# Homes of matmul operands modulo 128 bytes in a split-precision macaron block on one NeuronCore

## The chip, the cores and the metric

The kernel runs on one core of a Trainium2 chip. The metric is the device time of one execution in microseconds.

## The reference

One inference step of a diffusion backbone of two layers with `D_MODEL` 1024, on 128 context tokens and 512 latent tokens, all in float32. Each layer is a macaron block with adaLN modulation and norms on both sides:

```python
mod = adaln(c, w_mod[l], b_mod[l])
z = ffn_half(z, mod, 0, norm_w[l, 0], norm_w[l, 1], ffn_w1[l, 0], ffn_w2[l, 0])
h = modulate(rms_norm(z, norm_w[l, 2]), mod, 3)
q, k, v, gu, gv, pl = project(h, w_in[l])
...
out = merge_heads(attn, gu, gv, pl, w_spatial[l], b_spatial[l], w_pool[l], pool_scale[l], w_out[l])
z = z + mod[:, 5][:, None, :] * rms_norm(out, norm_w[l, 3])
z = ffn_half(z, mod, 6, norm_w[l, 4], norm_w[l, 5], ffn_w1[l, 1], ffn_w2[l, 1])
```

where `ffn_half` is x + 0.5 · gate · rms_norm(SwiGLU(h)), with `(silu(g) * u) @ w2` and [g, u] = h @ w1, and D_FF = 2816. The context tokens take the same path with weights in common and a conditioning vector of their own. The tokens' keys and values of the context are outputs too.

## The kernel before, in words

The tokens lie in five tiles of 128: group A holds tiles 0 and 1 (256 columns), group B tiles 2, 3 and 4 (384 columns; tile 4 is the context). There are six stages, three to a layer: 0, 2, 3 and 5 are feed-forward halves (`ffn_stage`), 1 and 4 are the mixing stages.

Every float32 operand of a matmul is split into a high part rounded to the format that TensorE multiplies and a low part, the difference (`split`, line 359: the high part on ACT at line 360, the low part on DVE at line 361). A product is then three matmuls that add into one PSUM bank: high by high, weight high by activation low, weight low by activation high. All of them are recorded at line 365 (`mm`), so the profile tells them apart by their operands: in `PS<-h0hi,whi` the first name is the moving operand (its columns stream through), the second the stationary one (it is loaded by an LDWEIGHTS, PEld in the profile).

The weights come by DMA into `raw`, are split into `whi` by ACT (line 328) and `wlo` by DVE (line 330), and wait in pools eight deep.

- The first product of a feed-forward half (`ffn1`, line 553): weight slices are stationary and the transposed, modulated tokens `h0` (group A) and `h1` (group B) move, as tiles of eight rows k of 256 or 384 columns in a high and a low part. For f in blocks of the hidden width, some f's run for group A alone ahead of the others (24 f's of 48 matmuls in all four stages together), while group B's tokens are still being made.
- In stages 2, 3 and 5, 49 blocks are done with seven products instead of eight (`ffn1_blocks`, line 657), which need sums of token parts: `S1` (256 columns) and `SZ` (384 columns), made by `sums`. Each product is twelve matmuls: products 0 and 1 use h0, 2 and 5 SZ, 3 S1, 4 and 6 h1.
- In stage 0 the f's that are not done for A alone take h0 and h1 in turn (15 f's of 48 of each), and `h1` is two columns wider there, for tokens whose shift comes late.
- The second product (`ffn2`, line 739, and `mm_tok`, line 698): the activations are stationary and the weights move, 512 columns at a time. The activation's high part `ahi` and low part `alo` are made by `ensure`: ahi in a pool of four, alo in the buffer of the previous activation (lines 759 and 760):

```python
hi = self.asp.tile([P, WB], F32R, name="ahi")
...
lo = self.ap.tile([P, wid], F32, name="alo", tag=f"act{g}{order[len(sp) - 1]}").bitcast(F32R)
...
def stat(f):
    ensure(order.index(f) + 1)
    return sp[f]
```

- The projections of the mixing stages use h0 and h1 as stationary operands, with moving weights.
- Beside the second products, DVE also adds up rows of the modulation matrices (line 434, `acc` from `wmt`), whose transfers are issued by SP (line 429).

The order on each engine is set by a scheduler that goes by priorities: each generator step gets a priority, and `sums` runs behind the stage's matmuls by `S_LAG` and `S_RATE` (line 38). Tiles are allocated in the order in which the pools and tags appear; `c1` is the pool of tiles that live for the whole program, `actp` the pool of activations of one stage. `new_h` (line 475) gives the tiles of h, and `boundary` (line 533) calls it at the end of a stage.

Of the kernel before, what the change touches and what calls it, by code (L numbers as in the profile page):

```python
# [8 lines left out]
F32 = mybir.dt.float32  # L9
F32R = mybir.dt.float32r  # L10
# [5 lines left out]
P = 128  # L16
D = 1024
KD = 8
# [5 lines left out]
GA = (0, 1)  # L24
GB = (2, 3, 4)
WA = 256
WB = 384
# [7 lines left out]
ADA_RATE2 = 0.7  # L35

BLOCKS = (2, 3, 5)
S_LAG, S_RATE = 30, 0.5
FREE = 1
MISC0 = (8, 9, 10, 11, 0, 1, 2, 3, 4, 5, 6, 7)  # L40
TAIL_A, TAIL_B, TAIL = 4, 1, 3
# [120 lines left out]
class Builder:  # L162
    def __init__(self, ctx, tc, a, n_stage=6):
        self.tc = tc
        self.nc = tc.nc
        self.a = a
        self.n_stage = n_stage
        pool = lambda name, bufs, **kw: ctx.enter_context(tc.tile_pool(name=name, bufs=bufs, **kw))
        self.c1 = pool("c1", 1)
        self.rawp = pool("raw", 5)  # L170
        self.wp = pool("wsp", 8)
        self.xp = pool("xp", 3)
        self.tmpp = pool("tmp", 4)
        self.stp = pool("st", 6)
        self.mdp = pool("md", 2)
        self.psp = pool("ps", 1, space=bass.MemoryType.PSUM)
        self.PS = self.psp.tile([P, 4096], F32, name="PS")
        self.ring = {}
        self.turn = {}
        self.drp = pool("dr", 1, space=bass.MemoryType.DRAM)  # L180
        self.xd = [self.drp.tile([P, D], F32, name=f"xd{t}", tag=f"xd{t}") for t in range(NT)]
        self.units = []
        self.plan()
        self.n_dma = 0
        self.n_split = 0
        self.n_use = 0
        self.dmas = []
        self.raws = {}
        self.spl = {}
        self.kept = {}  # L190
        self.pins = []
        self.lo_pool = 0
        self.xt = {}
        self.hT = {}
        self.md = {}
        self.rowd = {}
        self.pairs = {}
        self.kept_tmp = {}

    def bank(self, i):  # L200
# [175 lines left out]
    def setup(self):  # L376
        nc, a, c1 = self.nc, self.a, self.c1
        ct = c1.tile([P, C_W], F32, name="ct")
        cc = c1.tile([P, 2, KD], F32, name="cc")
        nc.sync.dma_start(cc[:, 0, :], a["c"].rearrange("b (p k) -> p (b k)", k=KD))  # L380
        nc.sync.dma_start(cc[:, 1, :], a["c_ctx"].rearrange("(p k) -> p k", k=KD))
        nc.sync.dma_start(ct[:, 0:C_COS], a["consts"][:, 0:C_COS])
        self.ident = ct[:, C_ID:C_ID + P]
        self.mhalf = ct[:, C_INVW + 2:C_INVW + 3]
        self.ct = ct
        self.identr = c1.tile([P, P], F32R, name="identr")
        nc.vector.tensor_copy(self.identr, self.ident)
        bf = c1.tile([P, 3, P], BF16, name="bf")
        nc.vector.tensor_copy(bf[:, 0, :], self.ident)
        self.bf = bf  # L390
        self.identb, self.maskL, self.maskR = bf[:, 0, :], bf[:, 1, :], bf[:, 2, :]
        self.ones = c1.tile([P, P], F32, name="ones")
        nc.vector.memset(self.ones, 1.0)
        self.cc = c1.tile([P, 2, KD], F32, name="ccs")
        nc.scalar.activation(self.cc, cc, AF.Silu)
        self.selc = c1.tile([P, 2], F32, name="selc")

    def setup_late(self):
        nc, a = self.nc, self.a
        mk = self.c1.tile([P, 2, P], F32, name="mk")  # L400
        nc.sync.dma_start(mk, a["consts"][:, C_ML:C_ALL].rearrange("p (a b) -> p a b", a=2))
        nc.sync.dma_start(self.ct[:, C_COS:C_W], a["consts"][:, C_COS:C_W])
        nc.vector.tensor_copy(self.bf[:, 1:3, :], mk)
        self.jk = mk.rearrange("p a b -> p (a b)").bitcast(BF16)
# [68 lines left out]
        self.nc.sync.dma_start(x, src)  # L473
        self.xt[t] = x

    def new_h(self, g):
        w = (WA, WB + 2)[g]
        return tuple(self.c1.tile([P, KD, w], F32R, name=f"h{g}{n}", tag=f"h{g}{n}") for n in ("hi", "lo"))

    def hcol(self, t):  # L480
        g = 0 if t in GA else 1
# [50 lines left out]

    def boundary(self, s, tiles, post, pre, cost, skew=3):
        if pre:
            self.hT[0 if tiles[0] in GA else 1] = self.new_h(0 if tiles[0] in GA else 1)
        gens = [self.bnd_steps(s, t, post, pre) for t in tiles]
        w = 0
        done = [False] * len(gens)
        while not all(done):
            for i, g in enumerate(gens):  # L540
                if not done[i] and w >= skew * i:
                    try:
                        next(g)
                    except StopIteration:
                        done[i] = True
            w += 1
            yield cost
# [194 lines left out]
    def ffn2(self, l, i, g, last=False):  # L742
        wid = (WA, WB)[g]
        sp = {}

        order = list(range(NF))
        if g:
            order = order[NF - KEEP_C:] + order[:NF - KEEP_C]

        def ensure(f):  # L750
            while len(sp) <= min(f, NF - 1):
                q = order[len(sp)]
                hi = self.asp.tile([P, WB], F32R, name="ahi")
                a = self.act[q, g]
                if len(sp):
                    lo = self.ap.tile([P, wid], F32, name="alo", tag=f"act{g}{order[len(sp) - 1]}").bitcast(F32R)
                else:
                    lo = self.asp.tile([P, WB], F32R, name="ahi")[:, 0:wid]
                self.nc.scalar.activation(hi[:, 0:wid], a, AF.Copy)  # L759
                self.nc.vector.tensor_tensor(lo, a, hi[:, 0:wid].bitcast(F32), ALU.subtract)  # L760
                sp[q] = (hi, lo)

        def stat(f):
            ensure(order.index(f) + 1)
            return sp[f]
        ensure(0)
        yield from self.mm_tok(lambda c, n: ("w2", l, i, c, n), (GA, GB)[g], order, stat, late=1 if g else 0, tail=(TAIL_A, TAIL_B, TAIL)[g + last])
# [523 lines left out]
    def ffn_stage(self, s, l, i, pend):  # L1291
        tc = self.tc
        last = s == self.n_stage - 1
        q = STG[s]
# [2 lines left out]
        early = list(range(max(0, na - KEEP_F)))  # L1297
        block = lambda pool, name: lambda *n: pool.tile([P, D], F32, name=name + "".join(map(str, n)))
        rows = [sum([self.rows(n) for n in ns if n < self.n_stage], []) for ns in ({0: (0, 1)}.get(s, ()), ADA_LATE[s])]
        with tc.tile_pool(name="actp", bufs=1, reuse_waits="tile") as ap, ExitStack() as late:  # L1300
            self.ap = ap

            def pools():
                self.asp, self.wmp, self.accsp = (late.enter_context(tc.tile_pool(name=n, bufs=b, reuse_waits="tile"))
                                                  for n, b in (("asp", 4), ("wmp", 3), ("accsp", 1)))
# [142 lines left out]
```

## Time and profile before

| | |
|---|---|
| median of 3 runs | 2399.22 us (2397.61 to 2403.58) |
| the profiled execution | 2398.8 us |
| its span | 2397.0 us |
| mean granted clock of TensorE | 0.993 |
| busy: TensorE / weight loads / DVE / ACT / GpSimd | 2317.4 / 2063.2 / 1829.1 / 1117.4 / 394.4 us |
| matmuls | 13304 |
| read from HBM, over the span | 341.50 MB, 149 GB/s with what is written |

The span is the time from the first to the last instruction that the profiler recorded; the execution's own time has 1.8 us more around it. TensorE's busy time is a modelled one: matmuls overlap, and a group's mean duration is longer than the time from one start to the next. To know what a matmul takes in a stream, one reads the starts in the timeline, not the durations.

### The profile page before, as it was taken

Reading aid. Unit: us, or ns where it says so; the run is one execution under the profiler, and the core shown is the slowest. Engines: PE = TensorE matmul, PEld = TensorE weight load, DVE = VectorE, ACT = ScalarE, POOL = GpSimd, SP = SyncE. Lnnn points to the kernel's source line nnn. Section 1 sums busy time; section 2 is a strip of 40 time slices with the busy share of each in tenths; the row PEclk is TensorE's granted clock in tenths of the full one; section 3 lists DMA queues with packets and bytes.
Section 4 is the critical chain, followed back from the end, with each engine's and each line's share of the span. In section 5 each row is a group of like instructions: output and inputs, shape, how many; then the busy total and the mean of one; then the engine's idle time right before and its main releaser. Section 6 shows DMA issues by size and latency. Waiting matters only on the chain.

```text
span 2397.0 us, 37303 instructions
## 1 busy us (share of the span) xinstructions
PE 2317.4 (97%) x13304; PEld 2063.2 (86%) x13304; DVE 1829.1 (76%) x2914; ACT 1117.4 (47%) x2309; POOL 394.4 (16%) x432
## 2 busy tenths in 40 slices
PE   8999999999999999999999999999999889999998
PEld 6999897777778999997789999877777789999887
DVE  5568678977776778889966888899958774788754
ACT  5422224444766444444453444544455563444543
POOL 2000000305324200000240000021545370000000
PEclk9999999999999999999999999999999999999999
DMA  9357667654325522348654222577622354222542
GB/s 295 113 174 242 197 194 249 230 163 127 107 71 155 170 80 80 88 137 266 219 181 121 86 82 80 197 227 245 213 73 62 106 172 137 75 85 71 187 156 93
DMA packets 330481, 360.07 MB, mean 150 GB/s; under 512 B 20451, under 2 KB 239843, under 8 KB 330294
## 3 DMA queue, kind: packets, MB, share of 16 engines
q1 hardware_dynamic: 326694, 344.58, 46.0%
q10 hardware_dynamic: 3600, 13.11, 1.4%
q8 instruction: 104, 1.70, 0.3%
q14 instruction: 83, 0.68, 0.1%
HBM read 341.50 MB, written 16.12 MB: 149 GB/s over the span
## 4 chain that ended last, share of the span: by engine, by line
PE 72%; DVE 13%; DMA 5%; issue 5%; POOL 2%; ACT 2%; SPq 1%; DVEq 0%; ACTq 0%; POOLq 0%
PE PS L365 70%; DVE wlo L330 3%; DVE acc L434 3%; DMA wmt<-in_w_mod 3%; DMA raw<-in_ffn_w 2%; DVE alo L760 1%; DVE ast L1057 1%; PE PS L443 1%; PE PS L1080 1%; POOL tmp L515 1%; DVE x L504 1%; DVE tl L361 1%; POOL wlo L330 0%; ACT pt L1063 0%; DVE h1lo L361 0%
## 5 line engine op out<-in xcount | busy, mean ns | idle before, releaser
L328 ACT ACTIVATE whi<-raw 128x512 fp32r<-128x512 f32 x668 | 417.0, 630 | 537.4 <-PE PS L365 387.8
L330 DVE TENSOR_TENSOR wlo<-raw,whi 128x512 fp32r<-128x512 f32 x614 | 455.4, 755 | 207.9 <-ACT whi L328 199.2
L365 PE MATMUL PS<-whi,ahi 128*128 128x512 f32 x920 | 354.6, 393 | 0.0
L365 PE MATMUL PS<-h1hi,whi 128*128 128x384 f32 (+1 forms) x1016 | 342.5, 338 | 2.2 <-ACT h1hi L360 2.1
L365 PE MATMUL PS<-h1hi,wlo 128*128 128x384 f32 (+1 forms) x1016 | 344.0, 339 | 0.0
L365 PE MATMUL PS<-h1lo,whi 128*128 128x384 f32 (+1 forms) x1016 | 343.4, 338 | 0.0
L365 PE MATMUL PS<-wlo,ahi 128*128 128x512 f32 x880 | 342.8, 391 | 0.0
L328 ACT ACTIVATE whi<-tmp 128x512 fp32r<-128x512 f32 x294 | 185.7, 633 | 256.7 <-PE PS L365 189.2
L365 PE MATMUL PS<-h0hi,whi 128*128 128x256 f32 x1016 | 289.7, 286 | 9.2 <-DVE act L596 8.6
L434 DVE SCALAR_TENSOR_TENSOR acc<-wmt,ccs,acc 128x1024 f32<-128x1024 f32 x224 | 279.7, 1278 | 24.3 <-DMA wmt<-in_w_mod 24.1
L365 PE MATMUL PS<-whi,alo 128*128 128x512 f32 x840 | 274.1, 396 | 21.0 <-DVE alo L760 21.0
L365 PE MATMUL PS<-h0hi,wlo 128*128 128x256 f32 x1016 | 289.2, 285 | 0.0
L365 PE MATMUL PS<-h0lo,whi 128*128 128x256 f32 x1016 | 288.9, 285 | 0.0
L330 DVE TENSOR_TENSOR wlo<-tmp,whi 128x512 fp32r<-128x512 f32 x294 | 201.5, 686 | 78.8 <-ACT whi L328 73.1
L365 PEld LDWEIGHTS PS<-whi,alo 128*128 128x128 f32 x840 | 155.0, 188 | 69.4 <-DVE alo L760 31.3
L365 PEld LDWEIGHTS PS<-h0hi,whi 128*128 128x128 f32 x1016 | 193.7, 191 | 20.0 <-DVE act L596 10.0
L365 PEld LDWEIGHTS PS<-whi,ahi 128*128 128x128 f32 x920 | 172.9, 188 | 39.5 <-ACT ahi L759 1.7
L365 PE MATMUL PS<-sz,whi 128*128 128x384 f32 x784 | 200.8, 337 | 0.0
L365 PEld LDWEIGHTS PS<-h0hi,wlo 128*128 128x128 f32 x1016 | 193.7, 191 | 4.3 <-issue 3.4
L365 PEld LDWEIGHTS PS<-wlo,ahi 128*128 128x128 f32 x880 | 165.3, 188 | 36.2
L365 PEld LDWEIGHTS PS<-h0lo,whi 128*128 128x128 f32 x1016 | 194.2, 191 | 1.8 <-issue 1.7
L365 PEld LDWEIGHTS PS<-h1hi,whi 128*128 128x128 f32 x1016 | 190.9, 188 | 2.8 <-ACT h1hi L360 2.8
(239 smaller groups left out, 4213.3 us busy)
## 6 DMA issues: line engine op xcount, KB each, us to landing
raw<-in_ffn_w SPq DMA_DIRECT2D x540, 256.0 KB
wmt<-in_w_mod SPq DMA_DIRECT2D x136, 512.0 KB
tmp<-in_ffn_w SPq DMA_DIRECT2D x98, 512.0 KB
raw<-in_w_in SPq DMA_DIRECT2D x80, 256.0 KB
xd<-x ACTq DMA_DIRECT2D x25, 512.0 KB
x<-xd SPq DMA_DIRECT2D x25, 512.0 KB
raw<-in_w_out SPq DMA_DIRECT2D x64, 128.0 KB
mdG<-rowG SPq DMA_DIRECT2D x12, 512.0 KB
```

The costliest lines, as they stand in the source:

```text
L328: self.nc.scalar.activation(hi, r, AF.Copy)
L330: eng.tensor_tensor(lo, r, hi.bitcast(F32), ALU.subtract)
L361: i1 = (eng or self.nc.vector).tensor_tensor(lo, src, hi.bitcast(F32), ALU.subtract)
L365: self.nc.tensor.matmul(out, w, m, start=start, stop=stop)
L434: nc.vector.scalar_tensor_tensor(accs[s], w, self.cc[:, s, k:k + 1], prev, ALU.mult, ALU.add)
L443: nc.tensor.matmul(ps[32 * q:32 * q + 32, :], self.ones[:, 0:32], accs[q // 2][:, 512 * (q % 2):512 * (q % 2) + 512], start=True, stop=Tru ...
L504: nc.vector.scalar_tensor_tensor(x, tmp, r, x, ALU.mult, ALU.add)
L515: nc.gpsimd.tensor_tensor(tmp[:, hs], tmp[:, hs], self.md["T", st][:, hs], ALU.add)
L760: self.nc.vector.tensor_tensor(lo, a, hi[:, 0:wid].bitcast(F32), ALU.subtract)
L1057: nc.vector.tensor_reduce(mx, S, AX.X, ALU.max)
L1080: nc.tensor.transpose(ps[:, w * c + P * j:w * c + P * j + P], pt[:, n * j + P * (c0 + c):n * j + P * (c0 + c) + P], self.ident)
```

## The change

There are three parts. First, it places three 64-byte tiles that nothing reads ("gap", "gap1", "gap2"), and makes the rows of h1 1536 bytes apart instead of 1544 (stage 0 keeps 1544). With this the addresses of the matmuls' operands within a partition, taken modulo 128 bytes, are as follows in the two built programs:

| operand | before | changed |
|---|---|---|
| weights `whi`, `wlo` | 64 | 64 |
| `h0`, high and low part | 64 | 0 |
| `h1`, high part, row k | 64 + 8k | 64 (stage 0: 64 + 8k) |
| `h1`, low part, row k | 8k | 64 (stage 0: 64 + 8k) |
| `S1` | 0 | 0 |
| `SZ` | 0 | 64 |
| activations, `ahi`, `alo` | 0 | 64 |
| `wmt`, `acc` | 0 | 64 |

Second, `ensure` is asked for activation parts two blocks ahead instead of one. Third, `S_LAG` and `S_RATE`, which set the priority of the token sums, go from 30 and 0.5 to 400 and 0.45.

```diff
--- before.py
+++ after.py
@@ -35,7 +35,7 @@
 ADA_RATE2 = 0.7
 
 BLOCKS = (2, 3, 5)
-S_LAG, S_RATE = 30, 0.5
+S_LAG, S_RATE = 400, 0.45
 FREE = 1
 MISC0 = (8, 9, 10, 11, 0, 1, 2, 3, 4, 5, 6, 7)
 TAIL_A, TAIL_B, TAIL = 4, 1, 3
@@ -195,6 +195,7 @@
         self.md = {}
         self.rowd = {}
         self.pairs = {}
+        self.gap = None
         self.kept_tmp = {}
 
     def bank(self, i):
@@ -394,6 +395,7 @@
         self.cc = c1.tile([P, 2, KD], F32, name="ccs")
         nc.scalar.activation(self.cc, cc, AF.Silu)
         self.selc = c1.tile([P, 2], F32, name="selc")
+        c1.tile([P, 16], F32, name="gap")
 
     def setup_late(self):
         nc, a = self.nc, self.a
@@ -473,9 +475,12 @@
         self.nc.sync.dma_start(x, src)
         self.xt[t] = x
 
-    def new_h(self, g):
-        w = (WA, WB + 2)[g]
-        return tuple(self.c1.tile([P, KD, w], F32R, name=f"h{g}{n}", tag=f"h{g}{n}") for n in ("hi", "lo"))
+    def new_h(self, g, late=False):
+        w = (WA, WB + 2 * late)[g]
+        if g == 1 and self.gap is None:
+            self.gap = self.c1.tile([P, 16], F32, name="gap1")
+        flat = [self.c1.tile([P, KD * (WA, WB + 4)[g]], F32R, name=f"h{g}{n}", tag=f"h{g}{n}") for n in ("hi", "lo")]
+        return tuple(v[:, 0:KD * w].rearrange("p (k q) -> p k q", k=KD) for v in flat)
 
     def hcol(self, t):
         g = 0 if t in GA else 1
@@ -532,7 +537,8 @@
 
     def boundary(self, s, tiles, post, pre, cost, skew=3):
         if pre:
-            self.hT[0 if tiles[0] in GA else 1] = self.new_h(0 if tiles[0] in GA else 1)
+            g = 0 if tiles[0] in GA else 1
+            self.hT[g] = self.new_h(g, not post)
         gens = [self.bnd_steps(s, t, post, pre) for t in tiles]
         w = 0
         done = [False] * len(gens)
@@ -761,7 +767,7 @@
                 sp[q] = (hi, lo)
 
         def stat(f):
-            ensure(order.index(f) + 1)
+            ensure(order.index(f) + 2)
             return sp[f]
         ensure(0)
         yield from self.mm_tok(lambda c, n: ("w2", l, i, c, n), (GA, GB)[g], order, stat, late=1 if g else 0, tail=(TAIL_A, TAIL_B, TAIL)[g + last])
@@ -1297,8 +1303,9 @@
         early = list(range(max(0, na - KEEP_F)))
         block = lambda pool, name: lambda *n: pool.tile([P, D], F32, name=name + "".join(map(str, n)))
         rows = [sum([self.rows(n) for n in ns if n < self.n_stage], []) for ns in ({0: (0, 1)}.get(s, ()), ADA_LATE[s])]
-        with tc.tile_pool(name="actp", bufs=1, reuse_waits="tile") as ap, ExitStack() as late:
+        with tc.tile_pool(name="gap", bufs=1, reuse_waits="tile") as gp, tc.tile_pool(name="actp", bufs=1, reuse_waits="tile") as ap, ExitStack() as late:
             self.ap = ap
+            gp.tile([P, 16], F32, name="gap2")
 
             def pools():
                 self.asp, self.wmp, self.accsp = (late.enter_context(tc.tile_pool(name=n, bufs=b, reuse_waits="tile"))
```

The order of the instructions on each engine, taken from the built programs, is the same before and in the change but for DVE and ACT at the start of stage 0. The line numbers of the changed program are up to six higher.

DVE at the start of stage 0, before; h1lo is the low part of group B's tokens, wlo that of a weight tile, and the rows on ahi and tmp belong to the late shift:

```order
28 L330 TENSOR_TENSOR wlo<-raw,whi 128x512 x4
29 L361 TENSOR_TENSOR h1lo<-PS,h1hi 128x4x128
30 L330 TENSOR_TENSOR wlo<-raw,whi 128x512 x5
31 L361 TENSOR_TENSOR acc_679<-acc_365,acc_679 99x512
32 L330 TENSOR_TENSOR wlo<-raw,whi 128x512
33 L361 TENSOR_TENSOR h1lo<-PS,h1hi 128x4x128
34 L330 TENSOR_TENSOR wlo<-raw,whi 128x512 x5
35 L361 TENSOR_TENSOR h1lo<-PS,h1hi 128x4x128 x3
36 L330 TENSOR_TENSOR wlo<-raw,whi 128x512
37 L1253 COPY ahi<-PS 128x16
38 L1266 SCALAR_TENSOR_TENSOR tmp<-h0hi,ahi,h0lo 128x256 x5
39 L361 TENSOR_TENSOR h1lo<-ahi,h1hi 128x8x2
```

The same place in the change:

```order
28 L331 TENSOR_TENSOR wlo<-raw,whi 128x512 x4
29 L362 TENSOR_TENSOR h1lo<-PS,h1hi 128x4x128
30 L331 TENSOR_TENSOR wlo<-raw,whi 128x512 x5
31 L362 TENSOR_TENSOR acc_684<-acc_370,acc_684 99x512
32 L331 TENSOR_TENSOR wlo<-raw,whi 128x512 x6
33 L362 TENSOR_TENSOR h1lo<-PS,h1hi 128x4x128 x4
34 L331 TENSOR_TENSOR wlo<-raw,whi 128x512
35 L1259 COPY ahi<-PS 128x16
36 L1272 SCALAR_TENSOR_TENSOR tmp<-h0hi,ahi,h0lo 128x256 x4
37 L362 TENSOR_TENSOR h1lo<-ahi,h1hi 128x8x2
```

The split of h1lo that stood alone between one and five splits of weights (row 33 before) now stands behind all six, together with the three others; one more h1lo split (128x8x2) has moved ahead of one of the five steps on tmp.

DVE in the ffn2 of stage 0, before; alo is the low part of an activation, acc a sum of modulation rows:

```order
276 L434 SCALAR_TENSOR_TENSOR acc_3743<-wmt,ccs 128x1024
277 L760 TENSOR_TENSOR alo<-act_261,ahi 128x256
278 L330 TENSOR_TENSOR wlo<-raw,whi 128x512 x2
279 L434 SCALAR_TENSOR_TENSOR acc_3742<-wmt,ccs,acc_3742 128x1024
280 L434 SCALAR_TENSOR_TENSOR acc_3743<-wmt,ccs,acc_3743 128x1024
281 L760 TENSOR_TENSOR alo<-act_263,ahi 128x256
282 L330 TENSOR_TENSOR wlo<-raw,whi 128x512 x3
283 L760 TENSOR_TENSOR alo<-act_265,ahi 128x256
```

The same place in the change:

```order
274 L436 SCALAR_TENSOR_TENSOR acc_3753<-wmt,ccs 128x1024
275 L766 TENSOR_TENSOR alo<-act_266,ahi 128x256
276 L331 TENSOR_TENSOR wlo<-raw,whi 128x512 x2
277 L436 SCALAR_TENSOR_TENSOR acc_3752<-wmt,ccs,acc_3752 128x1024
278 L436 SCALAR_TENSOR_TENSOR acc_3753<-wmt,ccs,acc_3753 128x1024
279 L766 TENSOR_TENSOR alo<-act_268,ahi 128x256
280 L331 TENSOR_TENSOR wlo<-raw,whi 128x512 x3
281 L766 TENSOR_TENSOR alo<-act_270,ahi 128x256
```

Nothing has moved: only the numbers in the names of buffers are higher, and each alo stands behind the same accumulation step and ahead of the same weight splits.

DVE in the group-B pass of stage 2, where the token sums are made, before; s and sz are S1 and SZ, and the step on act is part of a block's combination of products:

```order
740 L330 TENSOR_TENSOR wlo<-raw,whi 128x512
741 L642 TENSOR_TENSOR s_8621<-s_8621,h0lo 128x1024
742 L361 TENSOR_TENSOR h1lo<-PS,h1hi 128x4x128
743 L611 TENSOR_TENSOR tmp<-tmp,h0hi 128x512
744 L361 TENSOR_TENSOR sz_8236<-tmp,sz_8235 128x4x128
745 L596 TENSOR_TENSOR act_7753<-act_7753,PS 128x256
746 L529 TENSOR_TENSOR tmp<-tmp,PS 128x512
```

The same place in the change:

```order
738 L331 TENSOR_TENSOR wlo<-raw,whi 128x512
739 L648 TENSOR_TENSOR s_8632<-s_8632,h0lo 128x1024
740 L362 TENSOR_TENSOR h1lo<-PS,h1hi 128x4x128
741 L617 TENSOR_TENSOR tmp<-tmp,h0hi 128x512
742 L362 TENSOR_TENSOR sz_8247<-tmp,sz_8246 128x4x128
743 L602 TENSOR_TENSOR act_7764<-act_7764,PS 128x256
744 L534 TENSOR_TENSOR tmp<-tmp,PS 128x512
```

Here, too, only the numbers in the names differ.

## Rows read from the trace of the kernel before

**Rows 1.** The page: busy us, share, instructions; shares of the chain that ended last.

```profile
PE 2317.4 (97%) x13304; PEld 2063.2 (86%) x13304; DVE 1829.1 (76%) x2914; ACT 1117.4 (47%) x2309; POOL 394.4 (16%) x432
...
PE 72%; DVE 13%; DMA 5%; issue 5%; POOL 2%; ACT 2%; SPq 1%; DVEq 0%; ACTq 0%; POOLq 0%
```

**Rows 2.** TensorE's waits, by releaser: us in total, times, longest.

```profile
PE PS L365 <- DVE alo L760: 21.0, 22, 1.8
```

**Rows 3.** Stretches: length, busy PE, PEld, DVE, ACT, POOL; clock, DMA share, GB/s.

```profile
860.00:1060.00 200.00, 200.00 (x1331) 200.00 (x1330) 169.12 (x315) 95.39 (x191) 0.00 (x0) 1.00 0.28 79
430.00:500.00 70.00, 66.13 (x293) 50.90 (x295) 66.25 (x80) 30.57 (x58) 19.54 (x13) 1.00 0.66 218
2260.00:2390.00 130.00, 130.00 (x570) 106.66 (x569) 67.57 (x109) 55.45 (x109) 3.44 (x8) 1.00 0.41 132
```

**Rows 4.** Groups of TensorE: count | busy us, mean ns | idle before, releasers.

```profile
L365 PE MATMUL PS<-whi,ahi 128*128 128x512 f32 x920 | 354.6, 393 | 0.0
...
L365 PE MATMUL PS<-wlo,ahi 128*128 128x512 f32 x880 | 342.8, 391 | 0.0
L365 PE MATMUL PS<-h1hi,whi 128*128 128x384 f32 (+1 forms) x1016 | 342.5, 338 | 2.2 <-ACT h1hi L360 2.1
L365 PE MATMUL PS<-h0hi,whi 128*128 128x256 f32 x1016 | 289.7, 286 | 9.2 <-DVE act L596 8.6 <-ACT act L586 0.6
...
L365 PE MATMUL PS<-whi,alo 128*128 128x512 f32 x840 | 274.1, 396 | 21.0 <-DVE alo L760 21.0
L365 PE MATMUL PS<-sz,whi 128*128 128x384 f32 x784 | 200.8, 337 | 0.0
...
L365 PE MATMUL PS<-whi,h0hi 128*128 128x512 f32 x160 | 62.6, 409 | 5.4 <-ACT qf L887 2.6 <-DVE pl L883 1.6 <-ACT h0hi L360 1.0
```

**Rows 5.** Timeline of TensorE, S1 moving: start us, duration us, operation.

```profile
966.67 0.41 PE L365 MATMUL PS<-s,whi 128*128 128x256 f32 x2
...
967.03 0.39 PE L365 MATMUL PS<-s,whi 128*128 128x256 f32 x2
...
967.93 0.28 PE L365 MATMUL PS<-s,wlo 128*128 128x256 f32 x1
968.05 0.34 PE L365 MATMUL PS<-h1hi,whi 128*128 128x384 f32 x1
```

**Rows 6.** Timeline of TensorE, h0 moving, first and last of 95.

```profile
1981.44 0.28 PE L365 MATMUL PS<-h0lo,whi 128*128 128x256 f32 x1
...
1992.59 0.28 PE L365 MATMUL PS<-h0hi,wlo 128*128 128x256 f32 x1
```

**Rows 7.** Timeline, 512 columns: stationary h0, activations, h1; first and last of each.

```profile
535.58 0.40 PE L365 MATMUL PS<-wlo,h0hi 128*128 128x512 f32 x1
...
545.81 0.39 PE L365 MATMUL PS<-whi,h0hi 128*128 128x512 f32 x1
...
1106.78 0.63 PE L365 MATMUL PS<-whi,alo 128*128 128x512 f32 x2
...
1143.88 0.39 PE L365 MATMUL PS<-wlo,ahi 128*128 128x512 f32 x1
...
1919.17 0.40 PE L365 MATMUL PS<-whi,h1lo 128*128 128x512 f32 x1
...
1937.27 0.39 PE L365 MATMUL PS<-whi,h1lo 128*128 128x512 f32 x1
```

**Rows 8.** Timeline, 384 columns: h1 moving (first, last of 197), then SZ.

```profile
812.11 0.34 PE L365 MATMUL PS<-h1hi,whi 128*128 128x384 f32 x1
...
846.48 0.34 PE L365 MATMUL PS<-h1hi,whi 128*128 128x384 f32 x1
...
913.88 0.51 PE L365 MATMUL PS<-sz,whi 128*128 128x384 f32 x2
...
916.00 0.41 PE L365 MATMUL PS<-s,whi 128*128 128x256 f32 x2
```

**Rows 9.** The page's costliest groups: DVE's split of weights.

```profile
L330 DVE TENSOR_TENSOR wlo<-raw,whi 128x512 fp32r<-128x512 f32 x614 | 455.4, 755 | 207.9 <-ACT whi L328 199.2
```

## The prediction

> **What bounds the kernel now.** First the busy times and the chain that ended last [rows 1]: TensorE is busy for 2317.4 of the span's 2397.0 us, and 72% of the chain is its own work, with 13% of DVE and 5% of transfers. Where it works, little stops it, so what one matmul takes is the kernel's time. The second view is the list of what TensorE waits for. Its largest entry in the matmuls of line 365 is the low part of an activation, "alo" of line 760: 21.0 us in 22 waits [rows 2]. The third view, by stretches, tells which stages have room [rows 3]. In the seven-product blocks of stage 2 (860 to 1060 us) both TensorE and its weight loads are busy without a gap at a granted clock of 1.00, the 2.4 GHz level; in the last ffn2 (2260 to 2390) TensorE has no gap either; in the first ffn2 (430 to 500) it is busy for 66.13 of 70 us, and DVE for 66.25, so DVE sets the pace there. The fourth view groups the matmuls by operands [rows 4] and gives the counts below.
>
> The change names two homes, so the next thing to read is what one matmul takes at each. The durations in the groups overlap (a 256-column matmul shows 286 ns and the next starts after 119), so I read starts from the timeline, the distance from one start to the next.
> - 256 columns, S1 moving (home 0, weights at 64): three at 120 ns each, from 966.67 to 967.03, then nine in 1.02 us, 113.3 ns each [rows 5].
> - 256 columns, h0 moving (home 64, weights at 64): 94 intervals from 1981.44 to 1992.59, 118.6 ns each [rows 6].
> - 512 columns: activations stationary (home 0, weights moving at 64), 162 intervals from 1106.78 to 1143.88, 229.0 ns; h0 stationary (home 64), 44 intervals, 232.5 ns; h1 stationary (mixed homes), 78 intervals, 232.05 ns [rows 7].
> - 384 columns: h1 moving (mixed homes), 196 intervals, 175.4 ns; SZ moving (home 0), 12 in 2.12 us, 176.7 ns [rows 8].
>
> Equal columns, different times: the cheaper one of each pair has its two operands in opposite 64-byte halves of 128, the dearer one in the same half. At 384 columns the pairing shows nothing.
>
> **The change, part by part.** The sum is made against the profiled execution, 2398.8 us; the median of the runs is 0.4 us above it, too little to matter.
>
> 1. *h0 moves from 64 to 0, opposite to the weights.* It is then where S1 is now. There are 1016 matmuls of each of three products, 3048 [rows 4]: 1176 in blocks (49 blocks of 24), 1152 in the parts of group A alone (24 f's of 48), 720 in stage 0 where they alternate with h1. A block: 24 × 118.6 = 2846 ns now; as S1, 3 × 120 + 21 × 113.3 = 2739; 107 ns saved, × 49 = **−5.2 us**. TensorE has no gap in the blocks, so this is all on the path. Group A alone: 1152 × 5.3 ns = 6.1 us. But its end is where TensorE waits, 8.6 us for DVE's gate "act" of line 596 and 2.1 for h1hi [rows 4]; what is late next is the same product at the same time. The ends are 0 and −6.1; I take half, **−3.0**. In stage 0 an h0 matmul stands beside one of h1 and never repeats; ends 0 and 720 × 5.3 = −3.8; I take **0**, since the first three of S1 behind a matmul of another operand gain nothing either.
> 2. *The activation parts move from 0 to 64, to the half of the weights.* 920 + 880 + 840 = 2640 matmuls [rows 4] go from 229.0 to h0's 232.5: 3.5 ns each, 9.2 us if all is on the path, 2.3 a stage. The last ffn2 has no gap and pays its 2.3 whole. In the other three TensorE waits 21.0 us for DVE's alo [rows 2]: slower matmuls there use time that is waited anyway. Ends 0 and 6.9; I take a third, 2.3. Together **+4.6**.
> 3. *h0 stationary in the mixing stages*, 3 × 160 = 480 matmuls [rows 4], goes the other way, 480 × −3.5 = −1.7; some end at waits; **−1.2**.
> 4. *h1 and SZ to 64.* 3048 h1 matmuls and 1176 of SZ move, 384 columns, and 720 with h1 stationary. Both kinds lie at 175 to 177 ns now, whichever the home, so **0**. Upper end: 3048 × (176.7 − 175.4) = +4.0. Lower end: S1's settled rate by columns, 113.3 × 1.5 = 170.0, or 5.4 × 3048 = −16.5. I stand far from the latter because SZ is already opposite the weights, as S1 is, and doesn't get there.
> 5. *Activation parts two ahead, and the sums' lag.* In the order of the built programs every alo stands between the same accumulation steps and weight splits, and every sum between the same neighbours: **0**. What covers this is the full DVE [rows 3], whose queue is served in that order however early the request is made. If the request did come sooner, the 21.0 us would be the most to gain.
> 6. *The start of stage 0:* one h1lo split stands behind five more weight splits of 0.755 us [rows 9]. If TensorE waited for that split alone it would lose 3.8 us. But three h1lo splits stood behind the same five before and still do, and the pass needs all of them: **0**, with the weight parts sooner by one split.
> 7. No instruction, transfer or queue entry is added: the gaps are memory. The rows of h1 that are 1536 instead of 1544 bytes apart change no count; **0**.
>
> Sum: −5.2 − 3.0 + 4.6 − 1.2 = −4.8, so **2394.0 us**; its own range, from half of each uncertain term, 2390 to 2399. A measurement of this kernel can tell about 0.3% from no change, 7.2 us; this case lies within it.
>
> **The rivals.**
> *B, the stationary side is free.* All of ffn2's 6.9 us in three stages vanish in the 21.0 us of waits, and h0 gains everywhere: −5.2 − 6.1 − 1.7, half of stage 0's 3.8 (−1.9), +2.3 in the last stage: −12.6, **2386.2**. For it: alo's waits are three times the cost. Against: 22 waits among 1980 matmuls mean that most of those matmuls run in streaks, as the 162 intervals do, and the waits for act follow the early end of group A. With h1 settling as well it would go below 2380.
> *C, homes don't matter and the change does nothing.* The differences would come from what runs beside: then 2398.8. Against it stand 113.3 and 118.6 ns for the same 256 columns, both at the 2.4 GHz level. The Trainium skill speaks for C (TensorE: Matmul & The Clock Gate, "Step-by-step: what each phase is for"): one read port of SBUF feeds the moving operand and another one the weight load, so loading doesn't take bandwidth from the running matmul. If that were all, opposite and equal halves would cost alike; the rows of S1 and h0 disagree.
> *D, the predecessor decides; slower.* S1 settles behind SZ, and both are now at home 0. If a streak settles only behind a matmul of its own home, h0 (behind h1, at 64) gains nothing, and S1 (behind SZ, now at 64) goes from 115.0 (1.38 us over 12) to 118.6: 49 × 12 × 3.6 ns = +2.1. ffn2's cost, between the +4.6 taken and the full 9.2, is +6.9. Sum +9.0, **2407.8**. It decides if S1's group takes over 1.41 us in the changed trace and h0's stays at 118. Against it: S1 settles after three matmuls, so the predecessor's trace is short.
>
> **How the numbers follow.** The forecast A 0.38, B 0.36, C 0.08, D 0.18. Faster by over 0.3% is B, 0.36; within it are A and C, 0.46; slower is D, 0.18. The range 2379 to 2408 leaves out half of D (0.09) and a part of B where h1 settles too (0.06).
>
> **What would show it.** In the changed profile the h0 streak ahead of h1 should read 113 to 115 ns a start, the dense ffn2 232 to 233, h1 and SZ 175 to 177, h0 as stationary 229; alo's wait should fall from 21.0 to 14 to 19 us, and the waits for act rise to 10 to 13. Waits for alo under 10 us would speak for B or for an alo that does come sooner; an h0 streak at 118 or more makes the forecast wrong whatever the total; h1 at 170 makes it wrong to the fast side.

## The result, and the profile after

The changed kernel takes 2382.41 us (median of 6 runs, 2381.46 to 2385.23) against 2401.35 us before (6 runs): a ratio of 0.9923, 95% interval 0.991 to 0.9936. On two other occasions it came out at 0.9947 (0.9933 to 0.996) and 0.993 (0.9915 to 0.9944), so the gain is 0.5 to 0.8%, some 13 to 19 us. The forecast was 2394.0, in a range of 2379 to 2408.

The profiled execution of the changed kernel took 2385.23 us, the highest of its six, and the one before 2398.8: 13.6 us to be found in the trace. The page and the list of waits of the changed kernel, answering to [rows 1, 2, 4]:

```profile
PE 2300.2 (97%) x13304; PEld 2050.9 (86%) x13304; DVE 1827.1 (77%) x2914; ACT 1118.5 (47%) x2309; POOL 393.5 (17%) x432
...
PE 71%; DVE 13%; DMA 6%; issue 5%; POOL 2%; ACT 2%; SPq 1%; DVEq 0%; ACTq 0%; POOLq 0%
```

```profile
PE PS L366 <- DVE alo L766: 20.9, 17, 2.3
...
PE PS L366 <- DVE act L602: 7.4, 6, 2.5
...
PE PS L366 <- ACT h1hi L361: 6.4, 3, 2.5
```

TensorE is busy for the same share of a shorter span. The other engines' work is what it was (DVE 1827.1 for 1829.1 us, ACT 1118.5 for 1117.4). The wait for alo is 20.9 for 21.0 us, although every matmul of ffn2 has changed. The granted clock is 0.993 in both.

What one matmul takes is read from starts again, in the timeline of TensorE (start us, duration us, operation). h0 moving, 95 intervals, answering to [rows 6]:

```profile
1971.99 0.28 PE L366 MATMUL PS<-h0hi,whi 128*128 128x256 f32 x1
...
1983.18 0.28 PE L366 MATMUL PS<-h0hi,wlo 128*128 128x256 f32 x1
```

In the blocks h0 moves in two runs of twelve matmuls; each run's first start and the start of the operand that follows it, before:

```profile
2219.11 0.28 PE L365 MATMUL PS<-h0hi,whi 128*128 128x256 f32 x1
...
2220.53 0.34 PE L365 MATMUL PS<-h1lo,whi 128*128 128x384 f32 x1
...
2226.67 0.28 PE L365 MATMUL PS<-h0hi,whi 128*128 128x256 f32 x1
...
2228.10 0.51 PE L365 MATMUL PS<-sz,whi 128*128 128x384 f32 x2
```

and changed:

```profile
2207.25 0.28 PE L366 MATMUL PS<-h0hi,whi 128*128 128x256 f32 x1
...
2208.62 0.34 PE L366 MATMUL PS<-h1lo,whi 128*128 128x384 f32 x1
...
2214.74 0.28 PE L366 MATMUL PS<-h0hi,whi 128*128 128x256 f32 x1
...
2216.10 0.52 PE L366 MATMUL PS<-sz,whi 128*128 128x384 f32 x2
```

S1 moving, twelve matmuls up to the next operand, answering to [rows 5]:

```profile
2218.18 0.39 PE L366 MATMUL PS<-s,whi 128*128 128x256 f32 x2
...
2219.54 0.34 PE L366 MATMUL PS<-h1hi,whi 128*128 128x384 f32 x1
```

Activations stationary in ffn2, 160 intervals, and h0 stationary, 47, answering to [rows 7]:

```profile
1100.12 0.40 PE L366 MATMUL PS<-wlo,ahi 128*128 128x512 f32 x1
...
1136.39 0.39 PE L366 MATMUL PS<-whi,alo 128*128 128x512 f32 x1
```

```profile
530.69 0.39 PE L366 MATMUL PS<-whi,h0hi 128*128 128x512 f32 x1
...
541.45 0.39 PE L366 MATMUL PS<-whi,h0lo 128*128 128x512 f32 x1
```

SZ moving, twelve matmuls, and h1 moving, 214 intervals, answering to [rows 8]:

```profile
2203.62 0.52 PE L366 MATMUL PS<-sz,whi 128*128 128x384 f32 x2
...
2205.71 0.28 PE L366 MATMUL PS<-s,whi 128*128 128x256 f32 x1
```

```profile
804.76 0.34 PE L366 MATMUL PS<-h1hi,wlo 128*128 128x384 f32 x1
...
842.33 0.28 PE L366 MATMUL PS<-s,whi 128*128 128x256 f32 x1
```

Worked out from them: h0 ahead of h1 11.19 us / 95 = 117.8 ns (118.6 before); h0 in a block 1.42 + 1.43 = 2.85 us before and 1.37 + 1.36 = 2.73 changed (2.847 and 2.731 as the mean of 43 blocks); S1 1.36 / 12 = 113.3 from the first matmul on (115.0); ffn2 36.27 / 160 = **226.7** (229.0; the expectations below write 226.9); h0 stationary 10.76 / 47 = 228.9 (232.5); SZ 2.09 / 12 = 174.2 (176.7); h1 175.6 (175.4). The block of seven products, from one S1 to the next, before:

```profile
2217.55 0.41 PE L365 MATMUL PS<-s,whi 128*128 128x256 f32 x2
...
2230.22 0.41 PE L365 MATMUL PS<-s,whi 128*128 128x256 f32 x2
```

and changed:

```profile
2205.71 0.28 PE L366 MATMUL PS<-s,whi 128*128 128x256 f32 x1
...
2218.18 0.39 PE L366 MATMUL PS<-s,whi 128*128 128x256 f32 x2
```

12.67 us has become 12.47. Over all matmuls of the two traces I added up the distance from a start to the next less the columns at S1's settled rate (113.3 ns for 256). Distances up to 15 ns longer are what a matmul takes in a stream; what is longer is a wait. The matmuls with fewer columns, which are the rest of the sum, lie some 21 us below that rate in both:

| us above the settled rate | before | changed | |
|---|---|---|---|
| h0 moving | 15.7 | 6.5 | −9.1 |
| ffn2 | 3.0 | −2.3 | −5.3 |
| SZ | 6.4 | 4.3 | −2.1 |
| h1 moving | 18.0 | 16.5 | −1.4 |
| S1 | 1.0 | 0.0 | −1.0 |
| h0, h1 stationary | 6.2 | 4.9 | −1.3 |
| all, with the rest | 29.2 | 9.2 | −20.0 |
| waits | 188.8 | 195.3 | +6.5 |

20.0 us came out of the matmuls, and the waits are 6.5 longer: together the 13.5 by which the span is shorter.

### The profile page after: what moved, and what is told of

It is laid out like the page before. It is cut to its first block, busy times and chain, and to the rows that moved or that the text cites. A ratio compares the mean times of both kernels' runs of the same rounds, so it can differ in the third digit from the quotient of the medians.

```text
span 2383.5 us, 37305 instructions
## 1 busy us (share of the span) xinstructions
PE 2300.2 (97%) x13304; PEld 2050.9 (86%) x13304; DVE 1827.1 (77%) x2914; ACT 1118.5 (47%) x2309; POOL 393.5 (17%) x432
## 4 chain that ended last, share of the span: by engine, by line
PE 71%; DVE 13%; DMA 6%; issue 5%; POOL 2%; ACT 2%; SPq 1%; DVEq 0%; ACTq 0%; POOLq 0%
PE PS L366 69%; DVE wlo L331 3%; DMA wmt<-in_w_mod 3%; DVE acc L436 3%; DMA raw<-in_ffn_w 2%; DVE alo L766 1%; PE PS L445 1%; POOL tmp L520 1%; DVE ast L1063 1%; DVE x L509 1%; PE PS L1086 1%; DVE tl L362 1%; DVE h1lo L362 1%; POOL wlo L331 1%; ACT whi L329 0%
## 5 line engine op out<-in xcount | busy, mean ns | idle before, releaser
L366 PE MATMUL PS<-whi,alo 128*128 128x512 f32 x840 | 272.7, 395 | 21.2 <-DVE alo L766 20.9
L366 PEld LDWEIGHTS PS<-wlo,ahi 128*128 128x128 f32 x880 | 166.2, 189 | 34.7
```

The source lines that it names most:

```text
L366: self.nc.tensor.matmul(out, w, m, start=start, stop=stop)
```

## The experiments

After the result there were three theories. D: what a matmul takes goes with the distance (moving less stationary) of its operands' addresses modulo 256, 0 cheapest and 128 dearest. H: homes modulo 128 decide, as the change is described. O: the order parts, two blocks ahead and the sums' lag, brought the gain. The first four runs tell these apart; D then became W, one best distance for each width.

**Order parts undone** (e1_no_order):

```diff
-S_LAG, S_RATE = 400, 0.45
+S_LAG, S_RATE = 30, 0.5
...
-            ensure(order.index(f) + 2)
+            ensure(order.index(f) + 1)
```

> The changed kernel with the activation parts one ahead and S_LAG, S_RATE at 30 and 0.5 again; homes as changed. Theory D (what a matmul takes goes with the distance of its two operands' addresses modulo 256: 0 cheapest, 128 dearest, 64 and 192 between): 2382, within 3 us of the changed kernel, and the streaks at 226.9 ns (ffn2) and 113.3 ns (S1) as there. Rival H (homes modulo 128, as the change is described, decide): the same 2382. Rival O (the request two ahead and the sums' lag brought the gain): at least half of the gain goes, 2391 or more.

Measured: 2382.7 us, 0.9932 (0.9915 to 0.995), the block of seven products 12.473 us as in the changed kernel. O falls: without the second and third parts of the change the gain is the same within the interval.

**Activations 128 bytes further** (e2_act128): homes equal modulo 128, different modulo 256.

```diff
-            gp.tile([P, 16], F32, name="gap2")
+            gp.tile([P, 48], F32, name="gap2")
```

> The changed kernel with 128 bytes more ahead of the activations: activations, ahi, alo and SZ stay at 64 modulo 128 but lie 128 from the weights modulo 256. Theory D: dense ffn2 goes from 226.9 to 232.5 ns, 2640 x 5.6 = 14.8 us before waits, SZ from 173.4 to 175.5 or more, 1176 x 2.1 = 2.5; with a part lost in DVE's waits 2390 to 2400. Rival H: nothing changes, 2382.

Measured: 2398.33 us, 0.9998 (0.9986 to 1.0009): the gain is gone. The timeline of ffn2, first and last of 162 matmuls:

```profile
1105.10 0.39 PE L366 MATMUL PS<-whi,ahi 128*128 128x512 f32 x1
...
1142.51 0.40 PE L366 MATMUL PS<-whi,alo 128*128 128x512 f32 x1
```

37.41 us / 161 = 232.4 ns, for 226.7 at the same home modulo 128. H falls. This is also the forecast's mistake laid bare: in the built programs h0 stood at 192 modulo 256 and the weights at 64, 128 apart; they are in equal halves only modulo 128.

**h1lo to distance 0** (e3_h1lo, and again beside the changed kernel as e10_h1lo_again):

```diff
-        flat = [self.c1.tile([P, KD * (WA, WB + 4)[g]], F32R, name=f"h{g}{n}", tag=f"h{g}{n}") for n in ("hi", "lo")]
+        flat = [self.c1.tile([P, KD * (WA, WB + 8)[g]], F32R, name=f"h{g}{n}", tag=f"h{g}{n}") for n in ("hi", "lo")]
```

> The changed kernel with rows for h1 in a tile 128 bytes longer, so that h1lo, which lay 128 from the weights modulo 256, lies at distance 0 as h1hi does (outside stage 0). Theory D: h1 moving goes from 175.6 to 173.3 ns, 2082 x 2.2 = 4.6 us, h1 stationary from 231.3 to 226.9, 720 x 4.4 = 3.2; some of it lost in waits: 2375 to 2379. Rival H: 2382.

> The kernel of e3_h1lo beside the changed kernel on one chip. Theory W: its matmuls start 4.7 us sooner in sum (h1 at 173.4 instead of 175.6 ns), most of it in stretches without a wait, so 3 to 5 us below the changed kernel. Rival: as in ffn2, waits take it back, within 2 us.

Measured: 2379.49 us, 0.9919 (0.9906 to 0.9932), and 2379.94 us, 0.9917 (0.9905 to 0.9929), where the changed kernel beside it had 2383.9. The first lies just above the 2375 to 2379 that D expected, the second within the 3 to 5 us below the changed kernel that W expected. The same stream of h1 in the second of these runs, 214 intervals:

```profile
804.80 0.34 PE L366 MATMUL PS<-h1hi,wlo 128*128 128x384 f32 x1
...
841.90 0.28 PE L366 MATMUL PS<-s,whi 128*128 128x256 f32 x1
```

37.10 us / 214 = 173.4 ns for 175.6. The sum over all matmuls, as in the table above, fell from 8.6 us in the changed kernel beside it to 4.0. The medians say 4 us better than the changed kernel; the intervals of the two ratios overlap, so the runs show that it beats the kernel before, and make it likely, not certain, that it beats the change.

**h0 to distance 0** (e4_h0at64):

```diff
-        c1.tile([P, 16], F32, name="gap")
+        c1.tile([P, 32], F32, name="gap")
...
-        if g == 1 and self.gap is None:
-            self.gap = self.c1.tile([P, 16], F32, name="gap1")
```

> The changed kernel with h0 at 64 instead of 0, modulo 128 and 256 (all else in its place). Theory D: distance 0, so the streaks of group A alone go from 117.8 to 113.3 ns, 1152 x 4.4 = 5.1 us less what waits take, h0 stationary from 229.1 to 226.9, 480 x 2.2 = 1.1: 2377 to 2381. Rival H: h0 is back in the weights' half and at 118.6 ns, 1176 x 5.3 + 1152 x 0.8 = 7.2 more, 2389.

Measured: 2392.56 us, 0.9974 (0.9964 to 0.9984). The h0 stream, 96 intervals up to the first h1:

```profile
1980.76 0.28 PE L366 MATMUL PS<-h0hi,whi 128*128 128x256 f32 x1
...
1992.27 0.34 PE L366 MATMUL PS<-h1hi,whi 128*128 128x384 f32 x1
```

11.51 us / 96 = 119.9 ns. The distance that suits 384 and 512 columns best is no better for 256 than 128, where these streams took 118.6 to 119.9. D falls in this form, and H was right here by luck. h0 as stationary operand of 512 columns did go to 226.7 ns in the same run. So each width has its own best distance (W).

**Activations and SZ alone** (e5_act_only), the kernel before with the 64-byte tile ahead of `actp`:

```diff
-        with tc.tile_pool(name="actp", bufs=1, reuse_waits="tile") as ap, ExitStack() as late:
+        with tc.tile_pool(name="gap", bufs=1, reuse_waits="tile") as gp, tc.tile_pool(name="actp", bufs=1, reuse_waits="tile") as ap, ExitStack() as late:
             self.ap = ap
+            gp.tile([P, 16], F32, name="gap2")
```

and **h0 alone** (e6_h0_only), with 64 bytes ahead of h0 and 192 behind it, so that nothing else moves modulo 256:

```diff
+        c1.tile([P, 16], F32, name="gap")
...
+        if g == 1 and getattr(self, "gap", None) is None:
+            self.gap = self.c1.tile([P, 48], F32, name="gap1")
```

> The kernel before with the 64-byte tile ahead of the activations alone: activations, ahi, alo and SZ go to distance 0 from the weights, h0 and h1 stay. Theory W (each width has its own best distance modulo 256: 384 and 512 columns 0, 256 columns not 0): dense ffn2 229.0 to 226.9 ns, 2640 x 2.1 = 5.6 us, SZ 175.5 to 173.5, 1176 x 2.0 = 2.3, S1 0.9; with some lost in waits 6 to 9 us below the kernel before. The forecast's step (the weights' half costs 3.5 ns): up to 9 us above it.

> The kernel before with h0 alone moved, to 0, distance 192 from the weights as S1; all else where it was. Theory W: in blocks 118.6 to 113.3 ns, 5.2 us, in group A alone 119 to 117.8, 1.5, h0 stationary 232.5 to 229, 1.6: 6 to 9 us below the kernel before, and together with the run before it most of the change's gain. Rival: if h0 gains only because its neighbours h1 and SZ were moved too, less than 3 us.

> The changed kernel itself, on the chip of the other three, for the comparison: 2382 or 0.992 of the kernel before.

Measured beside one another: activations and SZ alone 2395.24 us, 0.9986 (0.9977 to 0.9994); h0 alone 2385.82, 0.9939 (0.9927 to 0.9952); the changed kernel 2387.47, 0.9947 (0.9933 to 0.996). Both expectations of 6 to 9 us were missed, one on each side: h0 alone gives as much as the whole change, and the activations little. The changed kernel, too, came out some 5 us above its 2382, so the three are compared with one another. With h0 alone, the h0 stream (96 intervals) and the block, by the timeline:

```profile
1967.70 0.28 PE L365 MATMUL PS<-h0hi,whi 128*128 128x256 f32 x1
...
1978.58 0.34 PE L365 MATMUL PS<-h1hi,whi 128*128 128x384 f32 x1
...
2200.96 0.28 PE L365 MATMUL PS<-s,whi 128*128 128x256 f32 x1
...
2213.43 0.28 PE L365 MATMUL PS<-s,whi 128*128 128x256 f32 x1
```

h0 runs at 10.88 / 96 = 113.3 ns here, and the block takes 12.47 us, the whole of the change's gain in the blocks, although SZ, S1 and h1 lie where they lay: SZ's second product went from 176.4 to 173.1 ns a start and S1 from 115.1 to 113.6 (from their starts in all blocks). A stream's rate depends on what ran before it, not on its own homes alone. The h0 stream ahead of stage 5's h1 says the same: h0 and the weights are as far apart modulo 256 here, in the changed kernel and in that of e10_h1lo_again, and the stream takes 113.3, 117.8 and again 113.3 ns (96 intervals of the last):

```profile
1970.36 0.28 PE L366 MATMUL PS<-h0hi,whi 128*128 128x256 f32 x1
...
1981.23 0.34 PE L366 MATMUL PS<-h1hi,whi 128*128 128x384 f32 x1
```

Each value came back in every trace of the same homes: 117.8 in e1_no_order, e7_after_again and e9_after too, 113.3 in e3_h1lo. The changed kernel and that of e10_h1lo_again differ modulo 256 only in the low part of h1. The activations alone shortened the matmuls by 8.1 us (29.2 to 21.1 in the sum above) and the time by 3.4. A part of the rest is looked for in the length of the four ffn2, first to last matmul, from the starts in the traces:

| us | stage 0 | stage 2 | stage 3 | stage 5 |
|---|---|---|---|---|
| before (229.0 ns) | 168.5 | 166.5 | 167.9 | 150.8 |
| h0 alone (228.9) | 163.9 | 165.6 | 168.5 | 150.8 |
| activations alone (226.7) | 166.5 | 166.3 | 168.7 | 149.4 |
| changed (226.7) | 166.2 | 167.6 | 168.9 | 149.4 |
| changed, e7_after_again | 165.6 | 167.4 | 167.8 | 149.4 |
| changed, e9_after | 165.2 | 166.8 | 166.9 | 149.4 |
| 128 further (232.4) | 167.0 | 168.4 | 170.9 | 153.1 |

The last ffn2 follows the matmul: from 228.9 to 226.7 ns in it, 660 × 2.2 is about 1.4 us, 150.8 to 149.4. The other three together last 502.9 us before, 498.0 with h0 alone, 501.5 with the activations alone, and 502.7, 500.8 and 498.9 in three traces of the changed kernel. The 4.3 us that three stages would gain do not show, but the changed kernel by itself scatters by 3.8. In these stages TensorE waits for alo, and the wait is 17.6 us with h0 alone

```profile
PE PS L365 <- DVE alo L763: 17.6, 18, 1.8
```

and 20.9 in the changed kernel, whose matmuls are faster. But it is 21.0 before, with the slow matmul, and 21.2 and 23.2 in the other two traces of the changed kernel. That the faster matmuls' gain is waited there is likely, and not shown.

**h0 64 beyond the weights** (e8_h0at128) and **32 short of them** (e12_h0at32), both on the kernel of e3_h1lo, by the sizes of the two tiles around h0 (48 and 48, then 24 and 8):

```diff
-        c1.tile([P, 16], F32, name="gap")
+        c1.tile([P, 48], F32, name="gap")
...
-            self.gap = self.c1.tile([P, 16], F32, name="gap1")
+            self.gap = self.c1.tile([P, 48], F32, name="gap1")
```

> The kernel of e3_h1lo with h0 at 128 modulo 256, 64 beyond the weights instead of 64 short of them. Theory W with only distance 0 bad for 256 columns: h0's streaks stay between 113.3 and 117.8 ns, 2379.5 within 3 us. Rival: the mirrored distance costs as much as 0 did, 120 ns in streaks, 2390.

> The kernel of e3_h1lo with h0 at 32, distance 224 modulo 256. Theory W with only distance 0 bad for 256 columns: streaks between 113.3 and 117.8 ns, within 3 us of e3_h1lo. Rival: what is bad for 256 columns is nearness to 0, so 32 short of the weights reads towards 120 ns, and 5 us or more above it.

Measured: 2382.45 us, 0.9932 (0.9919 to 0.9945), streams of h0 at 117.8 ns; and 2387.77 us, 0.9947 (0.9934 to 0.996), streams at 118.3 to 118.5. The first is as expected, the second misses: neither end of its expectation, 117.8 or 120, was met, and the time went the rival's way, 7.8 us above the run of e10_h1lo_again beside it. No other distance tried brought 256 columns to the 113.3 ns that 192 reached. In the last run h0 as stationary operand, 47 intervals, is at distance 32:

```profile
531.50 0.39 PE L366 MATMUL PS<-whi,h0hi 128*128 128x512 f32 x1
...
542.47 0.39 PE L366 MATMUL PS<-whi,h0lo 128*128 128x512 f32 x1
```

10.97 us / 47 = 233.4 ns, the dearest seen at 512 columns.

**h0, activations and SZ without h1's new rows** (e11_h0_act), the edits of e5_act_only and e6_h0_only together, beside the changed kernel run once more:

> The changed kernel once more, as the measure for the next three on their chip: 0.992 to 0.995 of the kernel before.

> The kernel before with h0 at distance 192 and the activations and SZ at distance 0, but h1 with its old rows. Theory W with waits: h1's new rows leave the mean of h1's matmuls where it was (175.6 for 175.4 ns), so this is the whole change: equal to the changed kernel within 3 us, and the three ffn2 beside DVE still last 165 to 169 us each. Rival: the rows of h1 bring half of the gain, 6 us or more above the changed kernel.

Measured: 2383.81 us, 0.9932 (0.992 to 0.9944), the changed kernel beside it 2383.9 us, 0.993. h1's rows are worth nothing that shows as they were changed: its high part came to distance 0 from the weights, its low part to 128, and h1's stream takes 175.6 ns for 175.4. With both at distance 0 (e10_h1lo_again) it takes 173.4.

## Why the prediction was right, and where it was not

The time lay in the range, and the sign was right. The likeliest case, within 0.3%, was not what happened: at 0.992 to 0.995 the kernel is in the range of rival B, 2386.2, reached by other terms than B's.

- *Step 1, h0.* Right in sign and size for the blocks: the 24 matmuls of a block went from 2.847 to 2.731 us, 116 ns, × 49 = 5.7 us for the 5.2 forecast. The forecast counted three slow starts to a block; h0 comes in two runs, and six would have made it 4.2, but most starts settle sooner. All of h0's matmuls gave 9.1 us, for 5.2 + 3.0. The rule behind it, opposite halves of 128, was right by luck: the gap set h0 down 192 from the weights modulo 256, as S1 is. At distance 64 (e8_h0at128), which is opposite modulo 128 as well, the 24 matmuls take 2.820 us. And the h0 stream ahead of h1 reads 117.8 ns, not the 113 to 115 that was to show the step; it is 0.2 short of what was to prove the forecast wrong.
- *Step 2, the activations.* **This step failed, in sign.** It took 232.5 ns from h0 stationary as the price of "the half of the weights", +9.2 us dense. The runs show −5.3: 226.7 ns. The two homes were read modulo 128, where h0 and the weights look alike; they were 128 apart modulo 256 (e2_act128 puts the activations there and gets 232.4). The other half of the step held as far as the traces tell: the last ffn2 follows the matmul, and in the other three nothing shows beyond the scatter, so the wrong sign cost some 4.6 + 1.4 = 6 us of forecast and not 14. The wait for alo, which was to fall to 14 to 19 us, stayed at 20.9; that for act, which was to rise to 10 to 13, fell from 8.6 to 7.4.
- *Step 3, h0 stationary.* Right: 232.5 to 228.9 ns; −1.0 us in the sum for the −1.2 forecast.
- *Step 4, h1 and SZ at zero.* Too small: SZ −2.1, h1 −1.4 and S1 −1.0 us, 4.5 together. That SZ "is already opposite the weights and doesn't get there" was a right reading with the wrong conclusion: for 384 columns distance 0 is the better one. And e6_h0_only shows that most of this comes with h0's move alone. So the core of rival D, that the predecessor bears on a stream's rate, is real, though its sign was wrong: S1's group fell to 1.36 us where D wanted over 1.41.
- *Steps 5 and 7, at zero.* Right within the intervals, by e1_no_order for the two order parts and by e11_h0_act for the rows. Step 6 was not tried by itself; the first ffn2 begins 2.3 us sooner than before, so nothing of its upper end of 3.8 us was seen.
- *Rival C*, that homes don't matter, falls: one build with 128 bytes more in one place costs 16 us (e2_act128). By the Trainium skill (TensorE: Matmul & The Clock Gate, "Step-by-step: what each phase is for") one port feeds the weight load and another the moving operand. No run here shows the ports, and none contradicts them; what rival C drew from them, that a matmul costs alike wherever its operands lie, is contradicted by 226.7 and 232.4 ns at 512 columns.

By its own steps the forecast's sum should have read −5.7 (h0 in blocks), −3.4 (h0 elsewhere), −1.4 (the last ffn2), −1.3 (h0 and h1 stationary), −4.5 (SZ, S1, h1): −16.3, against −13 to −19 measured. This takes every term but the three ffn2 as time gained; the waits of the traces are not accounted for one by one.

## What to carry to other kernels

Where a matmul's time in a stream differs between operands of equal width, compare their addresses modulo more than one power of two before calling one row the price of a home; two homes of the activations that agree modulo 128 were 5.7 ns apart (226.7 and 232.4). Take the price from an experiment with the same width, since here the best distance for 512 columns was among the worst for 256. Move one operand at a time: h0 alone gave as much as the whole change. And value a faster matmul stage by stage: of four ffn2 with as many matmuls, the one without waits gained what the arithmetic said, and in the three beside a full DVE no gain shows beyond their scatter.

## What the runs showed of the hardware that was not expected

Time from start to start in a stream of float32r matmuls at the 2.4 GHz level, by the distance (address moving less stationary, modulo 256 bytes):

| columns | 0 | 32 | 64 | 128 | 192 | 224 |
|---|---|---|---|---|---|---|
| 256 | 119.9 | | 117.8 | 118.6 to 119.9 | 113.3 or 117.8 | 118.3 |
| 384 | 173.3 | | | 176.4 | 173.1 to 176.5 | |
| 512 | 226.7 | 233.4 | 229.0 | 232.4 | 233.4 | |

(from the kernels e4, e8, before, changed and e6, e12; e10, e2, before and e6; changed, e12, before, e2, e8.) The same homes can give two rates: at distance 192 the h0 stream ahead of stage 5's h1 ran at 113.3 ns with h0 alone moved and at 117.8 in the changed kernel, and what differs is what ran before it, with h1, SZ and the activations at other homes. The best values are 17, 26 and 34 times 6.67 ns; that a stream settles into a step that repeats would be a guess. The weights `whi` and `wlo` lay at 64 modulo 256 in every kernel, so the runs don't tell a distance of two operands from a home of the other operand by itself. Why a distance suits one width and not another no run shows, and it stays open.
